# Where the wide tiles of a two-layer decoder trunk stand in SBUF: multiples of 512 bytes, with the small tiles together in front

## The chip, the cores and the metric

The kernel runs on one core of a Trainium2 chip. The metric is the device time of one launch in microseconds (us). The three runs of the kernel before took 2445.65, 2446.26 and 2448.31 us; their median is 2446.26 us.

## What is computed

Two decoder layers on 1,024 tokens of width 1,024, all in float32. Cut to what matters:

```python
proj = x @ w_in                                   # 1024 x 3592 columns
fq, fk, fv, f_logit, rq, rk, rv, rg = split(proj) # f_logit has 8 columns
fox = attention(fq, fk, fv, bias=cumsum(log_sigmoid(f_logit + b)))   # 8 heads of 64, causal
ret = silu(rg) * groupnorm(retention(rotary(rq), rotary(rk), rv))    # 4 heads of 128, chunks of 128
x = layernorm(ALPHA * x + concat(fox, ret) @ w_out)
x = layernorm(ALPHA * x + square(relu(x @ w_ff1)) @ w_ff2)           # hidden width 4096
```

## The kernel before

**Products of float32 in three passes.** Each operand of a large matmul is split into a high part (`hi`, an ACT cast at line 152) and a remainder (`lo`, a DVE subtraction at line 153). `mm3` (line 211) and the two `product` functions (`triple` at line 1053 belongs to the second) then issue three matmuls for every 128 rows of contraction: lo·hi, hi·lo and hi·hi. Each matmul has a stationary operand of 128 x 128, which a weight load brings in before it, and a moving operand of 256, 264 or 512 columns.

**The stages of a layer, with their pools.**

- `p1`: value projection (`project_values`: 256 columns with weights `va`, then 264 columns with weights `vb`, that is 256 values and the 8 forget logits), `forget_sums`, then `retention` for two pairs of heads, each with four projections of 256 columns. In these the weights move and the tokens are stationary. Last comes the first of four pairs of `project_qk`, where the weights are stationary and 512 tokens move.
- `p2`: attention, with the other three pairs of `project_qk` woven between its steps.
- `p3`: the output projection with `w_out` (512 columns, `mm3`) and the first layer norm.
- `p3` and `p4`: `feed_forward_in`, 16 blocks of seven half-size products of 12 matmuls each (a Strassen-like scheme), 512 columns, line 843: 16 x 7 x 12 = 1,344 matmuls a layer, 2,688 in all. The stationary operand is a weight in `whi` or `wlo`, the moving one is `xop`.
- `p5`: `feed_forward_out`, the same count of matmuls at line 1053, both operands from the pair `ehi`, `elo`.

`mm3` issues 1,536 matmuls of 512 columns: 2 layers x 4 pairs x 2 names x 2 halves x 24 = 768 in `project_qk`, and 2 layers x 2 halves x 8 token tiles x 24 = 768 for `w_out`. Of the 768 in `project_qk`, 2 x 96 are in `p1` and 2 x 288 in `p2`.

**The weights' ring.** `load_next` fetches one block of weights into a staging tile `wst` (two buffers) and splits it into `whi` and `wlo` (four buffers each). All blocks share these tiles, so that each buffer has the size of the largest one: `vb` with 4 x 264 columns, 4,224 bytes in each partition; every other block has 4,096 bytes or less. `weight` asks for a block and emits the next two (`AHEAD`).

**Order.** The order of the instructions on each engine is set by a planner that simulates the program; a buffer's next user waits until the last one is done with it. Pools `p1` to `p5` use the same room one after the other (`reuse_waits="tile"`: a tile waits only for the tiles that stood where it stands). All DMA issues but one kind go through SP's queue, in order.

**Addresses.** Tiles stand one behind the other in the order of the pools and of their first use, each size rounded up to 32 bytes. In the built program of the kernel before these are the bytes in a partition at which they start:

| tile | starts at | remainder by 256 |
|---|---|---|
| `cst`, `half` (8 bytes) | 1152, 3968 | 128, 128 |
| `act`, 11 buffers of 8,192 (tokens, `mix`, most of `xop`) | 4000 + 8192 n | 160 |
| `wst`, 2 buffers of 4,224 | 94112, 98336 | 160, 32 |
| `whi`, 4 buffers of 4,224 | 102560, 106784, 111008, 115232 | 160, 32, 160, 32 |
| `wlo`, 4 buffers of 4,224 | 119456, 123680, 127904, 132128 | 160, 32, 160, 32 |
| `p1` to `p5`; in `p3` the other `xop` | from 140448 | 160 |
| `ehi` and `elo` of `p5`, 6 buffers of 4,096 each | 157216 + 4096 n | 32, 32 |

Matmuls run on TensorE in the order of the program, so that each one of the trace can be given its addresses. Three products of 12 matmuls at line 843 in layer 1, by the time at which their first one starts in the trace:

| first matmul | moving `xop` | stationary `whi`, `wlo` | remainders by 256 |
|---|---|---|---|
| 2004.57 us | 61344, 44960 | 111008, 127904 | 160 and 160 |
| 2007.30 us | 4000, 36768 | 108832, 125728 | 160 and 32 |
| 2010.09 us | 69536, 12192 | 115232, 132128 | 160 and 32 |

(The product at 2007.30 uses the second half of its weights' tiles. Each of the three stretches has 12 matmuls, up to the next line or up to 2012.88 us. In a tile of weights each further 128 columns start 512 bytes later, in `xop` each further 512 columns 2,048 bytes later, which leaves the remainders as they are.)

In the 256-column projections of layer 0 the same can be done: of the matmuls of 256 columns, those from 98.21 us to 99.64 us move `whi` and `wlo` with remainder 32 past stationary tokens with 160, those from 99.64 us to 101.06 us with remainder 160 past 160, and then again 32 past 160.

Of the kernel before, what the change touches and what calls it, by code (L numbers as in the profile page):

```python
# [9 lines left out]
F32 = mybir.dt.float32  # L10
# [7 lines left out]
P = 128  # L18
# [21 lines left out]
LEAD_ORDER = (0, None, 1, None, 2, None, 3, None, 0, 1, 2, 3, 4, 5, 4, 5)  # L40
SPAN = 3.0
ACT_SLOTS = 11
RING = 4
# [31 lines left out]
def hybrid_trunk(ctx: ExitStack, tc, x, w_in, w_out, w_ff1, w_ff2, ln1_g, ln1_b, ln2_g, ln2_b,  # L75
# [3 lines left out]

    cp = ctx.enter_context(tc.tile_pool(name="cp", bufs=1))  # L80
    act = ctx.enter_context(tc.tile_pool(name="act", bufs=ACT_SLOTS))
    wp = ctx.enter_context(tc.tile_pool(name="wp", bufs=RING))
# [15 lines left out]
    V.tensor_copy(mbf, cst[:, 384:512])  # L98
    half = cp.tile([P, 2], F32, tag="half", name="half")
    V.memset(half, -0.5)  # L100

    q_d = dp.tile([FH, 2, FD, S], F32R, tag="q_d", name="q_d")
# [82 lines left out]
    place = {k: n for n, k in enumerate(order)}  # L185
    loaded, emitted = {}, [0]

    def load_next(after=None):
        key = order[emitted[0]]
        emitted[0] += 1  # L190
        src = specs[key]
        _, kk, cc = src.shape
        st = wp.tile([P, kk, cc], F32, tag="wst", name=nm("wst"), bufs=2)
        if after is not None:
            V.tensor_copy(st[0:1, 0, 0:1], after)
        SP.dma_start(st, src)
        hi = wp.tile([P, kk, cc], F32R, tag="whi", name=nm("whi"))
        lo = wp.tile([P, kk, cc], F32R, tag="wlo", name=nm("wlo"))
        split(hi, lo, st)
        loaded[key] = (hi, lo)  # L200
# [48 lines left out]

    def rstd_of(pool, mv, n):  # L250
        sd = pool.tile([P, n], F32, tag="sd", name=nm("sd"), bufs=2)
        G.tensor_scalar(sd, mv[:, :, 1], EPS, 1.0, op0=ALU.add, op1=ALU.mult)
        rs = pool.tile([P, n], F32, tag="rs", name=nm("rs"), bufs=2)
        G.tensor_tensor(rs, sd, half[:, 0:n], op=ALU.pow)
        nb = pool.tile([P, n], F32, tag="nb", name=nm("nb"), bufs=2)
        V.scalar_tensor_tensor(nb, mv[:, :, 0], -1.0, rs, op0=ALU.mult, op1=ALU.mult)
        return rs, nb

    def layernorm(pool, z, st, g, b):
        mv = pool.tile([P, 1, 2], F32, tag="mv", name=nm("mv"), bufs=2)  # L260
        V.bn_aggr(mv[:, 0, :], st)  # L261
        V.scalar_tensor_tensor(z, z, mv[:, 0, 0:1], g, op0=ALU.subtract, op1=ALU.mult)
        sd = pool.tile([P, 1], F32, tag="sd", name=nm("sd"), bufs=2)
        G.tensor_scalar(sd, mv[:, :, 1], EPS, 1.0, op0=ALU.add, op1=ALU.mult)  # L264
        rs = pool.tile([P, 1], F32, tag="rs", name=nm("rs"), bufs=2)
        G.tensor_tensor(rs, sd, half[:, 0:1], op=ALU.pow)
        V.scalar_tensor_tensor(z, z, rs, b, op0=ALU.mult, op1=ALU.add)

    def layernorm_halves(pool, z, st, g, b, dst):
        mv = pool.tile([P, 1, 2], F32, tag="mv", name=nm("mv"), bufs=2)  # L270
        V.bn_aggr(mv[:, 0, :], st)
        rs, nb = rstd_of(pool, mv, 1)
# [13 lines left out]

    def project_values(l, xT, pool, prepare):
        wv = [weight(l, "va", g) for g in range(2)]
# [18 lines left out]
        wv = [weight(l, "vb", g) for g in range(2)]  # L307
        bf = pool.tile([P, FH], F32, tag="bf", name=nm("bf"), bufs=1)
        SP.dma_start(bf, rows(b_forget[l], P))
        z = pool.tile([P, NT, FH], F32, tag="z", name=nm("z"), bufs=1)  # L310
        for tt in range(NT):
# [3 lines left out]
            V.tensor_tensor(z[:, tt, :], ps[:, 256:264], bf, op=ALU.add)  # L315
        return z

# [33 lines left out]
    def retention(l, r, xT, pool, cos, sin, gn, steps):  # L351
# [77 lines left out]
        def outputs(tp, j, vt, inner):  # L429
            tt = 2 * tp + j  # L430
            po = ps_pv.tile([P, 512], F32, tag="pv", name=nm("pv"))
            for h in range(2):
                hs = slice(h * P, h * P + P)
                PE.matmul(po[:, hs], inner[:, hs], vt[:, j, h, :], start=True, stop=tt == 0)
                if tt > 0:
                    PE.matmul(po[:, hs], qT[tp][:, h, j, :], states[tt][:, hs], start=False, stop=True)
            st = pool.tile([P, 2, 6], F32, tag="rst", name=nm("rst"), bufs=2)
            mv = pool.tile([P, 2, 2], F32, tag="rmv", name=nm("rmv"), bufs=2)
            for h in range(2):
                V.bn_stats(st[:, h, :], po[:, h * P : h * P + P])  # L440
                V.bn_aggr(mv[:, h, :], st[:, h, :])
            rs, nb = rstd_of(pool, mv, 2)
# [42 lines left out]
    def attention(pool, mixes, fill, need, take):  # L485
# [15 lines left out]
        def load_bias(h):  # L501
            ncb = pool.tile([P, S], F32, tag="ncb", name=nm("ncb"), bufs=1)
            SP.dma_start(ncb, rows(c_d[h], P))
            ref = pool.tile([P, 4], F32, tag="ref", name=nm("ref"), bufs=2)
            G.tensor_scalar(ref, ncb.rearrange("p (a b) -> p a b", b=256)[:, :, 0], -1.0, 1.0, op0=ALU.mult, op1=ALU.mult)
            sums[h] = (ncb, ref)
# [8 lines left out]
        def front(h, qq, probs):  # L515
# [3 lines left out]
            for rb in (2 * qq, 2 * qq + 1):  # L519
# [5 lines left out]
                for c0 in range(0, nw, cw):  # L525
# [10 lines left out]
                    m2 = pool.tile([P, 1], F32, tag="mx", name=nm("mx"), bufs=6)  # L536
# [5 lines left out]
                sm = pool.tile([P, 1], F32, tag="sm", name=nm("sm"), bufs=4)  # L542
                A.activation(sc[:, 0:ne], sc[:, 0:ne], AF.Exp, bias=mx, scale=-1.0, accum_out=sm)
                ri = pool.tile([P, 1], F32, tag="ri", name=nm("ri"), bufs=4)
                V.reciprocal(ri, sm)
# [95 lines left out]
    def layer(l, xT, nxt):  # L641
        src = x if l == 0 else x_d
        with tc.tile_pool(name=f"p1_{l}", bufs=1, reuse_waits="tile") as pool:
# [26 lines left out]
            SP.dma_start(gn, rows(ret_gn_g[l].rearrange("h d -> (h d)"), P))  # L670
            z = project_values(l, xT, pool, prepare)
            forget_sums(z, pool)
            steps = [0]
            for r in range(2):
                retention(l, r, xT, pool, cos, sin, gn, steps)
            for _ in project_qk(l, 0, xT):
                pass
            settle()
        mix = {}
# [40 lines left out]
        with tc.tile_pool(name=f"p3_{l}", bufs=1, reuse_waits="tile") as outer:  # L720
# [3 lines left out]
            with tc.tile_pool(name=f"p3a_{l}", bufs=1, reuse_waits="tile") as pool:  # L724
                acc = []
                for tt in range(NT):
# [7 lines left out]
                    acc.append(a)  # L734
                gT = pool.tile([P, 8], F32, tag="gT", name=nm("gT"))
                bT = pool.tile([P, 8], F32, tag="bT", name=nm("bT"))
                SP.dma_start(gT, ln1_g[l].rearrange("(k p) -> p k", p=P))
                SP.dma_start(bT, ln1_b[l].rearrange("(k p) -> p k", p=P))
                stats = pool.tile([P, NT, 2, 6], F32, tag="stats", name=nm("stats"))

# [17 lines left out]
                def norm(tt):  # L758
                    mv = pool.tile([P, 1, 2], F32, tag="mv", name=nm("mv"), bufs=2)
                    V.bn_aggr(mv[:, 0, :], stats[:, tt])  # L760
                    rs, nb = rstd_of(pool, mv, 1)
                    A.activation(acc[tt], acc[tt], AF.Identity, bias=nb, scale=rs)
# [250 lines left out]
    def feed_forward_out(l, operands, nxt):  # L1013
# [10 lines left out]

        stats = keep.tile([P, NT, 2, 6], F32, tag="stats2", name=nm("stats2"))
        acc = {}
# [54 lines left out]
        def finish(tt):  # L1081
# [4 lines left out]
            if nxt is None and tt == NT - 1:  # L1086
                layernorm_halves(keep, zt, stats[:, tt], g, b, out[tt * P : tt * P + P, :])
                return
            layernorm(keep, zt, stats[:, tt], g, b)
            if nxt is None:  # L1090
# [71 lines left out]
```

## Time and profile before

| | |
|---|---|
| median of 3 runs | 2446.26 us |
| the profiled execution's own time | 2446.42 us |
| span of its instructions | 2444.6 us |
| PE (matmuls) busy | 2395.4 us, 98% |
| DVE, ACT, POOL busy | 62%, 42%, 15% |
| DMA | 442.68 MB, mean 181 GB/s |

The span runs from the first to the last instruction; 1.8 us of the profiled time lie around it. A matmul counts as busy from its start to its modelled end, and a matmul starts before the one ahead of it has ended: at 512 columns the mean of one is some 390 ns, while starts follow each other at some 230 ns. What a matmul costs is therefore read from the distance of the starts, or from a stretch in which PE has no gap, divided by the number of matmuls in it.

### The profile page before, as it was taken

Reading aid. Unit: us, or ns where it says so; the run is one execution under the profiler, and the core shown is the slowest. Engines: PE = TensorE matmul, PEld = TensorE weight load, DVE = VectorE, ACT = ScalarE, POOL = GpSimd, SP = SyncE. Lnnn points to the kernel's source line nnn. Section 1 sums busy time; section 2 is a strip of 40 time slices with the busy share of each in tenths; the row PEclk is TensorE's granted clock in tenths of the full one; section 3 lists DMA queues with packets and bytes.
Section 4 is the critical chain, followed back from the end, with each engine's and each line's share of the span. In section 5 each row is a group of like instructions: output and inputs, shape, how many; then the busy total and the mean of one; then the engine's idle time right before and its main releaser. Section 6 shows DMA issues by size and latency. Waiting matters only on the chain. (4 is left out here: it accounts for less than half of the span.)

```text
span 2444.6 us, 35615 instructions
## 1 busy us (share of the span) xinstructions
PE 2395.4 (98%) x13424; PEld 2063.4 (84%) x13424; DVE 1521.2 (62%) x2720; ACT 1019.7 (42%) x1540; POOL 376.2 (15%) x661
## 2 busy tenths in 40 slices
PE   8999999999999999999999999999999999999997
PEld 8999977787788888888899998877877888888886
DVE  4655447854876667665755554577557766576557
ACT  3212246734544454334321222477264444443331
POOL 0324224600000000000203332245000000000003
PEclk9999999999999999999999999999999999999998
DMA  6555675433364458667545567664334544586664
GB/s 212 174 211 199 211 225 167 136 108 121 100 213 156 142 185 306 207 211 222 171 151 190 190 225 234 177 172 112 117 104 146 182 159 162 193 303 215 198 191 146
DMA packets 243309, 442.68 MB, mean 181 GB/s; under 512 B 25520, under 2 KB 127920, under 8 KB 234944
## 3 DMA queue, kind: packets, MB, share of 16 engines
q1 hardware_dynamic: 240832, 432.01, 54.0%
q10 hardware_dynamic: 2304, 8.39, 0.9%
q8 instruction: 106, 1.74, 0.3%
q14 instruction: 67, 0.55, 0.1%
HBM read 301.85 MB, written 138.48 MB: 180 GB/s over the span
## 5 line engine op out<-in xcount | busy, mean ns | idle before, releaser
L153 DVE TENSOR_TENSOR elo<-est,ehi 128x1024 fp32r<-128x1024 f32 x216 | 261.2, 1222 | 183.0 <-ACT ehi L152 182.2
L152 ACT CAST ehi<-est 128x1024 fp32r<-128x1024 f32 x216 | 226.6, 1054 | 343.8 <-PE pv L1053 120.8
L211 PE MATMUL mm<-whi,act 128*128 128x256 f32 (+2 forms) x1376 | 274.4, 293 | 1.0 <-DVE act L153 0.5
L211 PE MATMUL qk<-whi,act 128*128 128x256 f32 (+2 forms) x1376 | 273.1, 292 | 0.8 <-DVE act L153 0.8
L211 PEld LDWEIGHTS mm<-whi,act 128*128 128x128 f32 x1376 | 220.5, 191 | 5.5 <-ACT whi L152 0.8
L211 PEld LDWEIGHTS qk<-whi,act 128*128 128x128 f32 x1376 | 218.3, 189 | 4.6 <-DVE act L153 1.0
L152 ACT CAST whi<-wst 128x1024 fp32r<-128x1024 f32 (+2 forms) x156 | 132.4, 852 | 170.2 <-PE qk L211 55.6
L211 PE MATMUL mm<-wlo,act 128*128 128x256 f32 (+2 forms) x688 | 200.9, 292 | 0.7 <-DVE wlo L153 0.7
L264 POOL TENSOR_SCALAR sd<-mv 128x1 f32<-128x1 f32 x15 | 13.6, 908 | 1221.4 <-DVE mv L261 1221.1
L211 PE MATMUL qk<-wlo,act 128*128 128x256 f32 (+2 forms) x688 | 199.3, 290 | 0.0
L843 PE MATMUL qk<-xop,whi 128*128 128x512 f32 x608 | 189.8, 393 | 0.0
L153 DVE TENSOR_TENSOR wlo<-wst,whi 128x1024 fp32r<-128x1024 f32 (+2 forms) x156 | 153.0, 984 | 46.3 <-ACT whi L152 43.9
L211 PE MATMUL mm<-act,whi 128*128 128x512 f32 x512 | 166.4, 398 | 0.0
L843 PE MATMUL pv<-xop,whi 128*128 128x512 f32 x512 | 159.5, 393 | 0.0
L582 PE MATMUL pv<-pt,vp 128*128 128x256 f32 x640 | 130.9, 307 | 8.2 <-POOL pt L564 5.8
L843 PEld LDWEIGHTS qk<-xop,whi 128*128 128x128 f32 x608 | 114.5, 188 | 26.0
L211 PEld LDWEIGHTS mm<-wlo,act 128*128 128x128 f32 x688 | 131.2, 191 | 2.8 <-DVE wlo L153 1.0
L211 PEld LDWEIGHTS qk<-wlo,act 128*128 128x128 f32 x688 | 130.0, 189 | 1.6
L843 PE MATMUL mm<-xop,whi 128*128 128x512 f32 x384 | 119.5, 392 | 1.5 <-DVE xop L153 1.5
L152 ACT CAST pt<-tr 128x512 fp32r<-128x512 f32 (+1 forms) x160 | 85.7, 538 | 84.5 <-PE tr L559 79.6
L153 DVE TENSOR_TENSOR pt<-tr,pt 128x512 fp32r<-128x512 f32 (+1 forms) x160 | 99.8, 631 | 32.8 <-ACT pt L152 31.9
L843 PE MATMUL qk<-xop,wlo 128*128 128x512 f32 x304 | 120.1, 395 | 0.0
(260 smaller groups left out, 5628.8 us busy)
## 6 DMA issues: line engine op xcount, KB each, us to landing
est<-h_d SPq DMA_DIRECT2D x224, 256.0 KB, 3.7
wst<-in_w_ff_dram SPq DMA_DIRECT2D x76, 512.0 KB, 4.2
wr<-in_w_ff_dram SPq DMA_DIRECT2D x32, 1024.0 KB, 5.9
t_d<-ts SPq DMA_DIRECT2D x32, 1024.0 KB, 4.1
h_d<-hs SPq DMA_DIRECT2D x32, 1024.0 KB, 5.1
est<-t_d SPq DMA_DIRECT2D x128, 256.0 KB, 3.7
wst<-in_w_in_dram SPq DMA_DIRECT2D x52, 512.0 KB, 5.1
h_d<-rest SPq DMA_DIRECT2D x32, 768.0 KB, 5.6
```

The lines of the kernel that those rows point to most:

```text
L152: A.copy(hi, src)
L153: V.tensor_tensor(lo, src, hi.bitcast(F32), op=ALU.subtract)
L211: PE.matmul(ps, lhs(a, k), rhs(b, k), start=first and i == 0 and j == 0, stop=last and i == n - 1 and j == 2)
L264: G.tensor_scalar(sd, mv[:, :, 1], EPS, 1.0, op0=ALU.add, op1=ALU.mult)
L582: PE.matmul(ob[:, (qq % 2) * 256 : (qq % 2) * 256 + 256], vp[:, j, :], pt[b][:, 2 * i : 2 * i + 2, :], start=qq % 2 == 0 and jp == 0 and i ...
L843: PE.matmul(ps, ops[p][a][:, k, :], right[p][b][:, k, :], start=first and k == 0 and n == 0, stop=last and k == 3 and n == 2, skip_group_c ...
```

## The change

- The small tiles, those of 8 to 384 bytes (`sd`, `rs`, `nb`, `mv`, `rst`, `rmv`, `ref`, `mx`, `sm`, `ri`, `bf`, `gT`, `bT`, `stats`), leave the pools of the stages for a pool `sp` of their own, which stands ahead of `act` and lives as long as the kernel. The two `stats` become one.
- `half` gets 224 bytes in place of 8. With the sizes above, the tiles in front of `act` then end at byte 5,632 = 11 x 512 (1152 + 2304 + 256 + 256 + 224 for the constants, 1,440 for `sp`).
- The blocks `vb` no longer go through the ring: they get a staging tile `vst` of one buffer and tiles `vhi0`, `vlo0`, `vhi1`, `vlo1`, in a pool `p1v` that lives during `project_values` only. The ring's buffers shrink to 4,096 bytes. So `act`, `wst`, `whi`, `wlo`, `ev` and the pools `p1` to `p5` all start at multiples of 512.
- `p1` keeps `cos`, `sin`, `gn`, `z` (256 bytes) and `vt`; what `forget_sums` and `retention` use goes into a pool `p1r`, in the room of `p1v`. Both start 256 bytes past a multiple of 512. In `p1r` seven tiles of 256 bytes come first, so that its wide tiles stand at multiples of 512; those of `p1v` do not.

No instruction of any engine is added or taken away by the text of the program, and none changes its size.

```diff
+HALF_ROOM = 56
...
+    sp = ctx.enter_context(tc.tile_pool(name="sp", bufs=1))
     act = ctx.enter_context(tc.tile_pool(name="act", bufs=ACT_SLOTS))
     wp = ctx.enter_context(tc.tile_pool(name="wp", bufs=RING))
...
-    half = cp.tile([P, 2], F32, tag="half", name="half")
+    half = cp.tile([P, HALF_ROOM], F32, tag="half", name="half")[:, 0:2]
     V.memset(half, -0.5)
+
+    def small(shape, tag, bufs=2):
+        return sp.tile(shape, F32, tag=tag, name=nm(tag), bufs=bufs)
...
-        st = wp.tile([P, kk, cc], F32, tag="wst", name=nm("wst"), bufs=2)
+        odd = key[1] == "vb"
+        home, two = (odd_home[0], 1) if odd else (wp, 2)
+        tags = ("vst", f"vhi{key[2]}", f"vlo{key[2]}") if odd else ("wst", "whi", "wlo")
+        st = home.tile([P, kk, cc], F32, tag=tags[0], name=nm(tags[0]), bufs=two)
         if after is not None:
             V.tensor_copy(st[0:1, 0, 0:1], after)
         SP.dma_start(st, src)
-        hi = wp.tile([P, kk, cc], F32R, tag="whi", name=nm("whi"))
-        lo = wp.tile([P, kk, cc], F32R, tag="wlo", name=nm("wlo"))
+        hi = home.tile([P, kk, cc], F32R, tag=tags[1], name=nm(tags[1]))
+        lo = home.tile([P, kk, cc], F32R, tag=tags[2], name=nm(tags[2]))
         split(hi, lo, st)
...
-            st = pool.tile([P, 2, 6], F32, tag="rst", name=nm("rst"), bufs=2)
-            mv = pool.tile([P, 2, 2], F32, tag="rmv", name=nm("rmv"), bufs=2)
+            st = small([P, 2, 6], "rst")
+            mv = small([P, 2, 2], "rmv")
...
-            z = project_values(l, xT, pool, prepare)
-            forget_sums(z, pool)
-            steps = [0]
-            for r in range(2):
-                retention(l, r, xT, pool, cos, sin, gn, steps)
-            for _ in project_qk(l, 0, xT):
-                pass
-            settle()
+            z = pool.tile([P, NT, FH], F32, tag="z", name=nm("z"), bufs=1)
+            with tc.tile_pool(name=f"p1v_{l}", bufs=1, reuse_waits="tile") as odd_home[0]:
+                project_values(l, xT, pool, prepare, z)
+            with tc.tile_pool(name=f"p1r_{l}", bufs=1, reuse_waits="tile") as part:
+                forget_sums(z, part)
+                steps = [0]
+                for r in range(2):
+                    retention(l, r, xT, part, cos, sin, gn, steps)
+                for _ in project_qk(l, 0, xT):
+                    pass
+                settle()
...
-        stats = keep.tile([P, NT, 2, 6], F32, tag="stats2", name=nm("stats2"))
+        stats = small([P, NT, 2, 6], "stats", 1)
```

The remaining lines of the diff are of these kinds: a small tile is taken from `small`, and functions lose the argument `pool` for it.

## Rows read from the trace of the kernel before

**Rows 1.** The page: the span, and busy time of each engine.

```profile
span 2444.6 us, 35615 instructions
PE 2395.4 (98%) x13424; PEld 2063.4 (84%) x13424; DVE 1521.2 (62%) x2720; ACT 1019.7 (42%) x1540; POOL 376.2 (15%) x661
```

**Rows 2.** Waits of PE: in all, times, longest, in us.

```profile
PE tr L236 <- DMA xs<-in_x_dram: 6.1, 2, 5.0
PE pv L582 <- POOL pt L564: 5.8, 10, 1.2
PE mm L211 <- DVE ev L156: 3.5, 2, 1.9
```

**Rows 3.** Windows: length, busy us and instructions of each engine, granted clock, DMA.

```profile
740.00:880.00 140.00, 140.00 (x609) 114.18 (x607) 90.69 (x131) 68.69 (x104) 0.00 (x0) 1.00 0.41 145
1000.00:1140.00 140.00, 140.00 (x620) 115.91 (x619) 84.06 (x91) 55.45 (x53) 0.00 (x0) 1.00 0.66 200
1940.00:2080.00 140.00, 140.00 (x608) 114.17 (x607) 91.57 (x133) 67.23 (x101) 0.00 (x0) 1.00 0.45 162
2220.00:2360.00 140.00, 140.00 (x619) 115.96 (x618) 78.13 (x79) 53.96 (x52) 0.00 (x0) 1.00 0.68 206
```

**Rows 4.** Timeline of PE at line 843: start, length, engine, line, tiles.

```profile
2004.57 0.39 PE L843 MATMUL qk<-xop,wlo 128*128 128x512 f32 x1
...
2007.30 0.40 PE L843 MATMUL qk<-xop,wlo 128*128 128x512 f32 x1
...
2010.09 0.39 PE L843 MATMUL tr<-xop,wlo 128*128 128x512 f32 x1
...
2012.88 0.39 PE L843 MATMUL tr<-xop,wlo 128*128 128x512 f32 x1
```

**Rows 5.** Timeline of PE in the projections of 256 columns.

```profile
98.33 0.28 PE L211 MATMUL qk<-wlo,act 128*128 128x256 f32 x1
...
99.76 0.28 PE L211 MATMUL qk<-wlo,act 128*128 128x256 f32 x1
...
101.18 0.28 PE L211 MATMUL qk<-wlo,act 128*128 128x256 f32 x1
```

**Rows 6.** Windows, line 211 on PE alone, in the output projection.

```profile
535.00:575.00 40.00, 40.00 (x175) 1.00 0.42 144
```

**Rows 7.** Windows, PE alone, in the attention of either layer.

```profile
330.00:530.00 200.00, 192.14 (x1195) 1.00 0.48 135
1530.00:1740.00 210.00, 201.96 (x1236) 1.00 0.50 141
```

**Rows 8.** Timeline of SP and ACT: the first weights of layer 1.

```profile
1154.50 1.55 SPq L196 DMA_DIRECT2D wst<-in_w_in_dram  x2
1160.86 0.38 SPq L196 DMA_DIRECT2D wst<-in_w_in_dram  x1
1158.46 1.08 ACT L152 CAST whi<-wst 128x1056 fp32r<-128x1056 f32 x1 [2.38 <-DMA wst<-in_w_in_dram]
```

**Rows 9.** Timeline of PE: last matmul of layer 0, first with `vb`.

```profile
1221.25 0.40 PE L1053 MATMUL pv<-ehi 128*128 128x512 f32 x1
...
1249.98 0.28 PE L211 MATMUL mm<-whi,act 128*128 128x264 f32 x1
```

**Rows 10.** The page's DMA issues (us to landing), and a split of `vb`.

```profile
wst<-in_w_in_dram SPq DMA_DIRECT2D x52, 512.0 KB, 5.1
1159.57 1.26 DVE L153 TENSOR_TENSOR wlo<-wst,whi 128x1056 fp32r<-128x1056 f32 x1 [1.66 <-ACT whi L152]
```

**Rows 11.** Windows at the seam of the layers, all engines.

```profile
1217.00:1239.00 22.00, 20.58 (x153) 19.09 (x152) 20.79 (x31) 5.28 (x10) 5.49 (x8) 1.00 0.37 118
1239.00:1250.00 11.00, 11.00 (x95) 11.00 (x94) 1.46 (x4) 1.64 (x2) 0.00 (x0) 1.00 0.50 172
```

More of the change, by code (lines that the diff above doesn't have):

```diff
@@ L185, in hybrid_trunk @@
     place = {k: n for n, k in enumerate(order)}
-    loaded, emitted = {}, [0]
+    loaded, emitted, odd_home = {}, [0], [None]
     def load_next(after=None):
@@ L248, in transpose_half, with rstd_of, layernorm, layernorm_halves @@
             yield kk
-    def rstd_of(pool, mv, n):
-        sd = pool.tile([P, n], F32, tag="sd", name=nm("sd"), bufs=2)
+    def rstd_of(mv, n):
+        sd = small([P, 2], "sd")[:, 0:n]
         G.tensor_scalar(sd, mv[:, :, 1], EPS, 1.0, op0=ALU.add, op1=ALU.mult)
-        rs = pool.tile([P, n], F32, tag="rs", name=nm("rs"), bufs=2)
+        rs = small([P, 2], "rs")[:, 0:n]
         G.tensor_tensor(rs, sd, half[:, 0:n], op=ALU.pow)
-        nb = pool.tile([P, n], F32, tag="nb", name=nm("nb"), bufs=2)
+        nb = small([P, 2], "nb")[:, 0:n]
         V.scalar_tensor_tensor(nb, mv[:, :, 0], -1.0, rs, op0=ALU.mult, op1=ALU.mult)
         return rs, nb
-    def layernorm(pool, z, st, g, b):
-        mv = pool.tile([P, 1, 2], F32, tag="mv", name=nm("mv"), bufs=2)
+    def layernorm(z, st, g, b):
+        mv = small([P, 1, 2], "mv")
         V.bn_aggr(mv[:, 0, :], st)
         V.scalar_tensor_tensor(z, z, mv[:, 0, 0:1], g, op0=ALU.subtract, op1=ALU.mult)
-        sd = pool.tile([P, 1], F32, tag="sd", name=nm("sd"), bufs=2)
+        sd = small([P, 2], "sd")[:, 0:1]
         G.tensor_scalar(sd, mv[:, :, 1], EPS, 1.0, op0=ALU.add, op1=ALU.mult)
-        rs = pool.tile([P, 1], F32, tag="rs", name=nm("rs"), bufs=2)
+        rs = small([P, 2], "rs")[:, 0:1]
         G.tensor_tensor(rs, sd, half[:, 0:1], op=ALU.pow)
         V.scalar_tensor_tensor(z, z, rs, b, op0=ALU.mult, op1=ALU.add)
-    def layernorm_halves(pool, z, st, g, b, dst):
-        mv = pool.tile([P, 1, 2], F32, tag="mv", name=nm("mv"), bufs=2)
+    def layernorm_halves(z, st, g, b, dst):
+        mv = small([P, 1, 2], "mv")
         V.bn_aggr(mv[:, 0, :], st)
-        rs, nb = rstd_of(pool, mv, 1)
+        rs, nb = rstd_of(mv, 1)
         h0, h1 = slice(0, D // 2), slice(D // 2, D)
@@ L284, in rows, with project_values @@
         return ap.partition_broadcast(n)
-    def project_values(l, xT, pool, prepare):
+    def project_values(l, xT, pool, prepare, z):
         wv = [weight(l, "va", g) for g in range(2)]
@@ L307, in project_values @@
         wv = [weight(l, "vb", g) for g in range(2)]
-        bf = pool.tile([P, FH], F32, tag="bf", name=nm("bf"), bufs=1)
+        bf = small([P, FH], "bf", 1)
         SP.dma_start(bf, rows(b_forget[l], P))
-        z = pool.tile([P, NT, FH], F32, tag="z", name=nm("z"), bufs=1)
         for tt in range(NT):
@@ L441, in outputs @@
                 V.bn_aggr(mv[:, h, :], st[:, h, :])
-            rs, nb = rstd_of(pool, mv, 2)
+            rs, nb = rstd_of(mv, 2)
             on = pool.tile([P, 256], F32, tag="on", name=nm("on"), bufs=2)
@@ L503, in load_bias @@
             SP.dma_start(ncb, rows(c_d[h], P))
-            ref = pool.tile([P, 4], F32, tag="ref", name=nm("ref"), bufs=2)
+            ref = small([P, 4], "ref")
             G.tensor_scalar(ref, ncb.rearrange("p (a b) -> p a b", b=256)[:, :, 0], -1.0, 1.0, op0=ALU.mult, op1=ALU.mult)
@@ L535, in front @@
                         PE.matmul(ps[:, o : o + P], ibf, mbf, start=False, stop=True)
-                    m2 = pool.tile([P, 1], F32, tag="mx", name=nm("mx"), bufs=6)
+                    m2 = small([P, 1], "mx", 6)
                     V.tensor_tensor_reduce(out=sc[:, c0 : c0 + we], in0=ps[:, 0:we], in1=rel[:, c0 : c0 + we], scale=-1.0,
@@ L541, in front @@
                         yield
-                sm = pool.tile([P, 1], F32, tag="sm", name=nm("sm"), bufs=4)
+                sm = small([P, 1], "sm", 4)
                 A.activation(sc[:, 0:ne], sc[:, 0:ne], AF.Exp, bias=mx, scale=-1.0, accum_out=sm)
-                ri = pool.tile([P, 1], F32, tag="ri", name=nm("ri"), bufs=4)
+                ri = small([P, 1], "ri", 4)
                 V.reciprocal(ri, sm)
@@ L734, in layer @@
                     acc.append(a)
-                gT = pool.tile([P, 8], F32, tag="gT", name=nm("gT"))
-                bT = pool.tile([P, 8], F32, tag="bT", name=nm("bT"))
+                gT = small([P, 8], "gT", 1)
+                bT = small([P, 8], "bT", 1)
                 SP.dma_start(gT, ln1_g[l].rearrange("(k p) -> p k", p=P))
                 SP.dma_start(bT, ln1_b[l].rearrange("(k p) -> p k", p=P))
-                stats = pool.tile([P, NT, 2, 6], F32, tag="stats", name=nm("stats"))
+                stats = small([P, NT, 2, 6], "stats", 1)
                 def turn(hf):
@@ L758, in norm @@
                 def norm(tt):
-                    mv = pool.tile([P, 1, 2], F32, tag="mv", name=nm("mv"), bufs=2)
+                    mv = small([P, 1, 2], "mv")
                     V.bn_aggr(mv[:, 0, :], stats[:, tt])
-                    rs, nb = rstd_of(pool, mv, 1)
+                    rs, nb = rstd_of(mv, 1)
                     A.activation(acc[tt], acc[tt], AF.Identity, bias=nb, scale=rs)
@@ L1023, in affine @@
             return g, b
-        stats = keep.tile([P, NT, 2, 6], F32, tag="stats2", name=nm("stats2"))
+        stats = small([P, NT, 2, 6], "stats", 1)
         acc = {}
@@ L1086, in finish @@
             if nxt is None and tt == NT - 1:
-                layernorm_halves(keep, zt, stats[:, tt], g, b, out[tt * P : tt * P + P, :])
+                layernorm_halves(zt, stats[:, tt], g, b, out[tt * P : tt * P + P, :])
                 return
-            layernorm(keep, zt, stats[:, tt], g, b)
+            layernorm(zt, stats[:, tt], g, b)
             if nxt is None:
```

1 line of the change is left out of this document (removed).

## Prediction

> **What bounds the kernel now.** I read the page first: PE has matmuls in flight for 98% of the span, and no other engine is above 62% [rows 1]. The waits of PE come next: the longest kind sums to 6.1 us, at the very start, and the largest others are of 5.8 and 3.5 us [rows 2]. So the time is PE's own rate, and a change of where tiles stand can gain only if it changes that rate, and lose only if it makes PE wait.
>
> So the third view is windows, 140 us long, in the two feed-forward stages, where PE has no gap [rows 3]. Both stages issue the same matmul, 128 x 128 by 512 columns. In `feed_forward_in` a window holds 609 and 608 of them, in `feed_forward_out` 620 and 619. A matmul that reaches over the edge is counted in both windows, so I divide 140.39 us by the count: 230.5 and 230.9 ns against 226.4 and 226.8 ns. On average that is 230.7 against 226.6, or 4.1 ns each. The granted clock is 1.00 in all four. The faster stage moves more over DMA (share 0.66 and 0.68 against 0.41 and 0.45), so traffic does not explain the difference.
>
> The timeline inside `feed_forward_in` shows what does [rows 4]. Three stretches of 12 matmuls of the same line, engines and shapes take 2.73, 2.79 and 2.79 us: 227.5 ns each in the first, 232.5 in the other two. By the table of addresses, the first reads moving and stationary operand from starts with the same remainder by 256 (160 and 160), the others from different ones (160 and 32). In `feed_forward_out` both stand at 32, and it runs at the fast rate throughout. So neither remainder is slow by itself; equal is fast, unequal slow. The mean of 230.7 is a mixture, because the buffers of the ring are 4,224 bytes = 16.5 x 256 apart and alternate between the two remainders.
>
> **The change, part by part.**
>
> *Equal remainders at line 843.* Every wide tile but `vb` then starts at a multiple of 512, so all pairs are equal, as in `feed_forward_out`. I take its rate: 2,688 x 4.1 ns = **11.0 us** less [rows 3]. The bounds: 0 if the remainder is not the cause, and 11.6 at the fastest window's 226.4 ns, below which no row goes.
>
> *Equal remainders at 512 columns of `mm3`.* Half the ring's buffers again stand against tokens at 160. In the output projection 175 matmuls take 40.39 us, 230.8 ns, so 4.2 ns above the fast rate [rows 3, 6]. For the 768 of `w_out` and the 192 of `project_qk` in `p1`, where PE is dense, that is 960 x 4.2 = **4.0 us**. The other 576 lie in attention, where PE is busy 96% [rows 7] and some of what they save is waited away at the next step of the softmax. At 4.2 ns they are worth 2.4 us; I take half, **1.2 us**, with 0 and 2.4 as bounds.
>
> *256 and 264 columns.* In the projections 12 matmuls with unequal remainders take 1.43 us and 12 with equal ones 1.42 us: 119 ns either way [rows 5]. I cost this at **0**. The weights `vb` keep odd starts, and their 264 columns are in the same regime: 0. The transposes against `cst` (which stays at 1152) and the retention's matmuls are 128 columns, nearer to rows 5 than to rows 4: 0, with 1 us either way.
>
> *A pool for small tiles.* It removes some reuse waits on DVE and POOL, which have spare time [rows 1]: 0.
>
> *`vb` in tiles of its own.* In layer 0 `vst` waits for nothing. In layer 1 the cover shrinks. Before, the ring was free, and the last block of `vb` was cast at 1158.46 us [rows 8], 91 us ahead of its first use at 1249.98 us [rows 9]. Now `vst` and `vhi0` stand on the room of `est` and the first buffers of `ehi` in `p5`. By the order in which the ring is filled, one of these is read by the last group of four blocks, hence until the last matmul of layer 0 at 1221.25 us [rows 9]. From there one block takes 5.1 us to land, 1.08 for the cast and 1.26 for the subtraction [rows 8, 10], 7.4 us; the second waits for the single `vst`, so both are there after 14.9 us, at 1236.4 us, 13.6 us before their use. What is queued behind them: on SP the stores of layer 0's last rows and the tables for rotary, which are needed later; on ACT and DVE the evictions of transposed tokens, which PE needs at once. DVE is busy 20.79 of 22 us there [rows 11], so its two subtractions (2.5 us) may push an eviction back. PE already loses 22.0 - 20.58 = 1.4 us at that place. I take **+1.0 us**, with 0 and 4.7 (both casts and subtractions, 2 x 2.34, all in front of PE's evictions) as bounds.
>
> *The planner's order.* Freed ring buffers let `rq` be fetched earlier, and the planner may arrange other steps anew. The trace cannot show it. All of PE's idle time is 2444.6 - 2395.4 = 49 us [rows 1], so I allow a tenth of it, 5 us, either way, and take 0.
>
> Sum: -11.0 - 4.0 - 1.2 + 1.0 = -15.2 us on the profiled execution's own 2446.42 us (span 2444.6 and 1.8 around it), that is 2431.2. The median of the runs is 2446.26, 0.16 us lower; I say **2431 us**, 0.6% less.
>
> A rule of the Trainium skill speaks against this. The page "SBUF — State Buffer", section "Who interferes with whom", gives PE two independent read ports, one for the moving operand and one for the weight load, and says "PE and ACT never wait on anyone". By that rule the place of one operand against the other could not matter, and the sum would be 0: 2446 us. Rows 4 disagree with it, 227.5 against 232.5 ns in one stage, and the measurement decides; no run here yet changes the address alone.
>
> **The rivals.**
>
> *No change of rate: 2446 us (2443 to 2449).* The fast and slow stretches would differ by something that goes with the tile and not with its start, for example how lately DVE wrote it. For it: `feed_forward_in` has more DVE and ACT work than `feed_forward_out` (90.69 and 68.69 against 84.06 and 55.45 us in 140) [rows 3]. Against it: rows 4 switch rate exactly where the remainder switches, within 10 us of the same mixture of work.
>
> *The gain is given back in part: 2434 to 2441 us.* PE gets ahead of the splits and of attention's chain, or the seam costs its 4.7 us and the new order 5 more. For it: DVE at the seam [rows 11]. Against it: DVE and ACT have a third and half of `feed_forward_in` free [rows 3], and PE's gain is under 2%.
>
> *Slower: remainder 0 is the slow case.* Every fast stretch has both starts 32 bytes past a multiple of 128; nothing shows two starts at 0. If the reads then met at each step, all 512-column matmuls would run at 232.5 ns: 2 x 2,688 x 232.5 against 2,688 x (230.7 + 226.6) is +20.7 us, and 1,536 x 1.7 makes +2.6: 2470 us. It decides once the new rate is above 229.1 ns, the mean over all 6,912 of these matmuls now (2,688 at 230.7, 2,688 at 226.6, 1,536 at 230.8). Against it: equal remainders of 160 and of 32 are both fast.
>
> *Better still: under 2424 us.* The whole 2.4 us in attention, no loss at the seam and 5 us by a better order give 2424; a rate below 226.4 ns is on no row.
>
> **How the numbers follow.** Chances: forecast as summed (2425 to 2434) 0.68; given back in part 0.14; no change of rate 0.08; slower, by remainder 0 or by a seam and an order far worse than bounded, 0.07; better than 2425, 0.03. The first two make 0.82; their bounds are 2424 (the sum with every gain) and 2441, and that is the range. A measurement of this kernel can tell about 0.2%, or 4.9 us, from no change. The first two and the last fall under 2441.4, and a little of the "no change" case does too: faster 0.86; same 0.07; slower 0.07.
>
> **What would show it.** In the profile after: windows of 140 us in `feed_forward_in` should hold 619 or 620 matmuls, as `feed_forward_out` does, which itself stays as it is; products of 12 should all take 2.72 to 2.73 us; 256 columns stay at 119 ns. At the seam the load of `vb` should be issued after the last matmul of layer 0 and PE's idle time between the layers should grow by no more than some us. I am wrong if windows in `feed_forward_in` still hold 609, if `feed_forward_out` slows down, or if PE's waits grow by 10 us or more while its rate improves.

## The result, and the profile after

The changed kernel takes **2431.8 us** (median of 6 runs, 2428.72 to 2434.84), the kernel before 2446.5 in the same comparison (6 runs, 2445.09 to 2448.57). The ratio is 0.9938 with a 95% interval of 0.9925 to 0.9951: faster by 0.6%, where 2431 (2424 to 2441) was forecast. The profiled execution took 2434.84 us, 11.6 less than the profiled one before (2446.42). In the code after, line 843 is 853, 1053 is 1063, 211 is 220, 152 and 153 are 158 and 159, and 582 is 589.

The page of the changed kernel, span and busy time [rows 1]:

```profile
span 2433.1 us, 35602 instructions
PE 2383.8 (98%) x13424; PEld 2065.2 (85%) x13424; DVE 1520.0 (62%) x2720; ACT 1019.9 (42%) x1540; POOL 376.1 (15%) x661
```

PE (TensorE, which runs the matmuls; DVE, ACT and POOL are VectorE, ScalarE and GpSimd) is still the bound at 98%, with the same 13,424 matmuls; it is busy for 11.6 us less, and the span is 11.5 us shorter. So the matmuls themselves became faster, as the windows show. Windows of the changed kernel, in the columns of [rows 3], two in each feed-forward stage:

```profile
740.00:880.00 140.00, 140.00 (x620) 115.95 (x619) 91.87 (x136) 68.95 (x105) 0.00 (x0) 1.00 0.43 155
1000.00:1140.00 140.00, 140.00 (x620) 115.95 (x619) 80.97 (x85) 55.71 (x53) 0.00 (x0) 1.00 0.68 206
1930.00:2070.00 140.00, 140.00 (x619) 115.93 (x618) 92.89 (x135) 69.26 (x104) 0.00 (x0) 1.00 0.46 165
2210.00:2350.00 140.00, 140.00 (x620) 115.95 (x619) 76.73 (x78) 54.77 (x52) 0.00 (x0) 1.00 0.68 206
```

`feed_forward_in` (first and third row) now holds 620 and 619 matmuls where it held 609 and 608; `feed_forward_out` is as it was. The granted clock is 1.00 in all, before and after. The timeline of PE in the changed kernel, with the first matmuls of two products and of the one behind them [rows 4]:

```profile
2000.28 0.39 PE L853 MATMUL tr<-xop,wlo 128*128 128x512 f32 x1
...
2003.00 0.39 PE L853 MATMUL tr<-xop,wlo 128*128 128x512 f32 x1
...
2005.72 0.39 PE L853 MATMUL pv<-xop,wlo 128*128 128x512 f32 x1
```

Twelve matmuls take 2.72 us each time; the stretches of 2.79 us are gone. The output projection, line 220 on PE alone, in the columns of [rows 6]:

```profile
535.00:575.00 40.00, 40.00 (x179) 1.00 0.40 149
```

Here 179 matmuls start where 175 did. Not everything gained. The stretch from 232 to 252 us holds only matmuls of 256 columns in either kernel; first the kernel before, then the changed one:

```profile
232.00:252.00 20.00, 20.00 (x171) 1.00 0.58 205
```

```profile
232.00:252.00 20.00, 20.00 (x169) 1.00 0.58 198
```

With the 0.28 us of the one at the edge that is 20.28/171 = 118.6 ns before and 20.28/169 = 120.0 ns after: these became slower.

For the whole run I add up, in each trace, the distances from the start of a matmul to the start of the next, by line and width. Waits are in these sums.

| matmuls | before, us | after, us | difference | forecast |
|---|---|---|---|---|
| `feed_forward_in`, 2,688 | 627.3 | 616.7 | -10.6 | -11.0 |
| `mm3`, 512 columns, 1,536 | 364.6 | 361.0 | -3.6 | -5.2 |
| `mm3`, 256 columns, 3,456 | 421.1 | 424.0 | +2.9 | 0 |
| `feed_forward_out`, 2,687 | 609.4 | 609.7 | +0.2 | 0 |
| all others | | | -0.4 | +1.0 |
| all | | | -11.5 | -15.2 |

The seam of the layers, SP's queue in the changed kernel [rows 8 to 10]:

```profile
1220.03 9.02 SPq L1103 DMA_DIRECT2D x_d<-acc  x4
1229.14 0.39 SPq L675 DMA_DIRECT2D cos<-rope_dram  x1
...
1231.95 0.43 SPq L205 DMA_DIRECT2D vst<-in_w_in_dram  x1
...
1240.30 0.37 SPq L205 DMA_DIRECT2D vst<-in_w_in_dram  x1
```

DVE's subtractions for the two blocks, and PE's last matmul of layer 0 and first with `vhi`:

```profile
1239.02 1.26 DVE L159 TENSOR_TENSOR vlo<-vst,vhi 128x1056 fp32r<-128x1056 f32 x1 [5.05 <-ACT vhi L158]
...
1245.70 1.26 DVE L159 TENSOR_TENSOR vlo<-vst,vhi 128x1056 fp32r<-128x1056 f32 x1 [4.83 <-ACT vhi L158]
```

```profile
1215.59 0.39 PE L1063 MATMUL pv<-ehi 128*128 128x512 f32 x1
...
1244.44 0.28 PE L220 MATMUL mm<-vhi,act 128*128 128x264 f32 x1
```

The load of the first block left 16.4 us after the last matmul of layer 0, behind the stores of layer 0's last rows and the rotary tables, and the blocks were split by 1240.28 and 1246.96 us, the first 4.2 us ahead of the first matmul that needs it. PE paid nothing: the windows of 50 us around the seam, before and after, at the same place of the work, are

```profile
1215.00:1265.00 50.00, 48.58 (x379) 46.74 (x378) 27.12 (x43) 10.25 (x19) 5.49 (x8) 1.00 0.43 143
```

```profile
1210.00:1260.00 50.00, 48.62 (x380) 46.90 (x379) 28.98 (x45) 12.27 (x21) 5.49 (x8) 1.00 0.49 159
```

and PE's only waits in either are one of 0.8 and one of 0.5 us for DVE's tokens `act`.

### The profile page after: what moved, and what is told of

It is laid out like the page before. It is cut to its first block, busy times and chain, and to the rows that moved or that the text cites. A ratio compares the mean times of both kernels' runs of the same rounds, so it can differ in the third digit from the quotient of the medians.

```text
span 2433.1 us, 35602 instructions
## 1 busy us (share of the span) xinstructions
PE 2383.8 (98%) x13424; PEld 2065.2 (85%) x13424; DVE 1520.0 (62%) x2720; ACT 1019.9 (42%) x1540; POOL 376.1 (15%) x661
## 3 DMA queue, kind: packets, MB, share of 16 engines
q10 hardware_dynamic: 2304, 8.39, 0.8%
## 5 line engine op out<-in xcount | busy, mean ns | idle before, releaser
L220 PE MATMUL mm<-whi,act 128*128 128x256 f32 (+1 forms) x1248 | 251.0, 295 | 0.8 <-DVE act L159 0.5
L220 PE MATMUL qk<-whi,act 128*128 128x256 f32 (+1 forms) x1248 | 249.8, 294 | 0.8 <-DVE act L159 0.8
L220 PEld LDWEIGHTS mm<-whi,act 128*128 128x128 f32 x1248 | 202.1, 193 | 5.1 <-DVE act L159 0.8
L220 PEld LDWEIGHTS qk<-whi,act 128*128 128x128 f32 x1248 | 200.2, 191 | 4.4 <-DVE act L159 1.0
L158 ACT CAST whi<-wst 128x1024 fp32r<-128x1024 f32 (+1 forms) x152 | 128.3, 847 | 161.5 <-PE qk L220 46.7
L220 PE MATMUL mm<-wlo,act 128*128 128x256 f32 (+1 forms) x624 | 183.5, 294 | 0.7 <-DVE wlo L159 0.7
L220 PE MATMUL qk<-wlo,act 128*128 128x256 f32 (+1 forms) x624 | 181.9, 292 | 0.0
L159 DVE TENSOR_TENSOR wlo<-wst,whi 128x1024 fp32r<-128x1024 f32 (+1 forms) x152 | 148.2, 978 | 38.8 <-ACT whi L158 36.4
L220 PEld LDWEIGHTS mm<-wlo,act 128*128 128x128 f32 x624 | 120.6, 193 | 2.7 <-DVE wlo L159 1.0
L220 PEld LDWEIGHTS qk<-wlo,act 128*128 128x128 f32 x624 | 119.5, 191 | 1.5
L853 PE MATMUL qk<-xop,wlo 128*128 128x512 f32 x304 | 118.6, 390 | 0.0
```

Source lines behind the costliest of these rows:

```text
L158: A.copy(hi, src)
L159: V.tensor_tensor(lo, src, hi.bitcast(F32), op=ALU.subtract)
L220: PE.matmul(ps, lhs(a, k), rhs(b, k), start=first and i == 0 and j == 0, stop=last and i == n - 1 and j == 2)
L853: PE.matmul(ps, ops[p][a][:, k, :], right[p][b][:, k, :], start=first and k == 0 and n == 0, stop=last and k == 3 and n == 2, skip_group_c ...
```

## The experiments

**The theory:** a matmul of 512 columns runs at some 227 ns when the byte addresses of its moving and its stationary operand are equal by 256, and slower when they are not; nothing else of the change matters. **The rivals:** it is the multiple of 512 itself that helps; it is the pool for small tiles, or the new order of the work. Later a second question came up, what the places do at 256 columns. Times stand beside runs of the kernel before on the same chip: 2445.37 us (median of 20) for the first four kernels, 2446.53 (15) for the next four, 2445.6 (11) for the last three. Windows are of PE alone, 740 to 880 us (`feed_forward_in`) unless another stretch is named; columns are length, busy us and matmuls, granted clock, DMA share, GB/s. Where bytes are named, they come from the addresses in the built program.

**Everything 32 bytes past a multiple of 512.**

```diff
-HALF_ROOM = 56
+HALF_ROOM = 64
```

> The changed kernel with 32 bytes more in front of act: every wide tile starts 32 bytes past a multiple of 512, and the order of all instructions stays. Theory A (the remainders by 256 of the moving and the stationary operand must be equal): 140 us of feed_forward_in hold 619 or 620 matmuls as now, 2432 us (2429 to 2435). Theory B (the tiles must stand at multiples of 512): the rate falls back to that of the kernel before, 609 in 140 us, 2446 us. Open beside it: the 256-column matmuls take about 1 ns more in the changed kernel than before (3,456 of them, some 3 us); if that comes from starts at remainder 0, it goes away here and the time is 2429 us.

Measured: 2436.2 us (9 runs, 2434.73 to 2440.68), ratio 0.9963 (0.9951 to 0.9975).

```profile
740.00:880.00 140.00, 140.00 (x619) 1.00 0.40 145
```

The rate is that of the changed kernel: `feed_forward_in` sums to 617.0 us against 616.7. No wide tile stands at a multiple of 512, so that rival falls. The 4 us between this median and the changed kernel's may be noise: in the repeat on this chip, further down, the changed kernel took 2433.73 us, with an interval that overlaps this one. In the two profiles the difference is not in the rate; it lies in `mm3` at 512 columns in and around attention (176.6 us for `w_out` against 176.4, 188.5 for `project_qk` against 184.5), where waits are included. PE's wait for `ev` at the hand-over from `p1` to `p2` (in all, times, longest) and the window from 319 to 325 us behind it, here and then in the changed kernel:

```profile
PE mm L220 <- DVE ev L162: 4.8, 2, 2.6
319.00:325.00 6.00, 6.00 (x14) 0.50 1.02 246
```

```profile
PE mm L220 <- DVE ev L162: 3.6, 2, 2.0
319.00:325.00 6.00, 6.00 (x28) 1.00 1.02 245
```

So here PE waited 1.2 us longer, and behind the wait, at a granted clock of 0.50, 14 matmuls started where 28 did. The missing 14 are worth 14 x 0.229 = 3.2 us, an estimate from these rows and the 229 ns of dense starts in `project_qk`. The two together come to about the 4 us; why the wait was longer, these runs do not show.

**`vb` in tiles of its own, and nothing else.** The kernel before, with these lines of the change; the small tiles stay in their stages' pools, and tokens, ring and pools start 416 bytes past a multiple of 512, remainder 160.

```diff
+        odd = key[1] == "vb"
+        home, two = (odd_home[0], 1) if odd else (wp, 2)
+        tags = ("vst", f"vhi{key[2]}", f"vlo{key[2]}") if odd else ("wst", "whi", "wlo")
...
+            with tc.tile_pool(name=f"p1v_{l}", bufs=1, reuse_waits="tile") as odd_home[0]:
+                project_values(l, xT, pool, prepare, z)
```

> The kernel before with one part of the change alone: vb in tiles of its own, so that the ring's buffers are 4,096 bytes; the small tiles stay where they were. act, the ring and the pools then start at 416 past a multiple of 512 (remainder 160 by 256), nothing wide stands at a multiple of 512. Theory A: all pairs equal, 619 or 620 matmuls in 140 us, the whole gain, 2431 us (2428 to 2435). Theory B: 609 in 140 us, 2446 us. Theory C (the gain comes from the pool of small tiles, by fewer waits): 2446 us.

Measured: 2436.37 us (6 runs, 2431.91 to 2438.33), ratio 0.9958 (0.9941 to 0.9974), an interval that overlaps the changed kernel's.

```profile
740.00:880.00 140.00, 140.00 (x619) 1.00 0.43 155
```

Sums: 616.9 us for `feed_forward_in`, 361.7 for `mm3` at 512 columns, 423.0 at 256. This part alone, which makes the ring's buffers 16 x 256 bytes in place of 16.5, gives the whole change of rate. What the small tiles' pool adds to it is not told from nothing.

**The weights moved against the rest.** The changed kernel, with a tile of `SHIFT` bytes between `wst` and `whi` and one of `256 - SHIFT` behind `wlo`, so that only the weights move. Four sizes, 128, 64, 32 and 96:

```diff
+        if not odd and not padded:
+            padded.append(pad("pad1", SHIFT))
         hi = home.tile([P, kk, cc], F32R, tag=tags[1], name=nm(tags[1]))
         lo = home.tile([P, kk, cc], F32R, tag=tags[2], name=nm(tags[2]))
+        if not odd and len(padded) == 1:
+            padded.append(pad("pad2", 256 - SHIFT))
```

> The changed kernel with 128 bytes of padding between the staging tiles and whi, and 128 behind wlo: the weights' ring stands at remainder 128 by 256, everything else at 0. Theory A: every matmul of feed_forward_in and of mm3 is unequal; 2,688 x 5.9 ns = 15.9 us and 1,536 x 5.9 ns less what attention hides, 6 to 9 us, on 2432: 2455 us, slower than the kernel before (2446), with 603 to 605 matmuls in 140 us of feed_forward_in and still 620 in feed_forward_out. Theory B: half the operands stand at multiples of 512, so between 2432 and 2446. If the address does not matter: 2432.

> The same with 64 and 192 bytes of padding: the ring at remainder 64, the rest at 0. If any unequal pair is slow: as with 128, 603 to 605 matmuls in 140 us. If only the distance of 128 is slow: 619 or 620.

> The weights' ring at remainder 32, everything else at 0. Theory A (only equal is fast at 512 columns): 601 to 605 matmuls of feed_forward_in in 140 us. If reads are told apart by lines of 64 bytes, 32 counts as equal and it holds 619 or 620. The 256-column matmuls, which went from 424.0 us in all (remainder equal) to 419.6 (128 apart) and 415.3 (64 apart): between 415 and 424.

> The weights' ring at remainder 96, everything else at 0. Theory A: 601 to 605 matmuls of feed_forward_in in 140 us; if 32 and 96 differ from 64 and 128, the rule is one of steps of 64. The 256-column matmuls: between 415 and 424 us.

At 128 it took 2449.86 us (10 runs), ratio 1.002 (1.0008 to 1.0031): a little slower than before the change. The other three ran once: 2447.14 (64), 2448.51 (32) and 2461.19 us (96). `feed_forward_in` and `feed_forward_out` at 128:

```profile
740.00:880.00 140.00, 140.00 (x601) 1.00 0.40 145
1000.00:1140.00 140.00, 140.00 (x619) 1.00 0.65 200
```

The stage whose operands were moved apart falls to 601 matmuls, (140 + 0.39)/601 = 233.6 ns; the one whose operands both stay where they were keeps 619. At 64, 32 and 96 the first row holds 602, 601 and 600. So any of the four distances costs, and in this stage about the same. Mean distances of starts over the whole run, gaps beyond 260 ns (145 ns at 256 columns) left out:

| weights past tokens by | `feed_forward_in`, ns | `w_out`, ns | `mm3` 256 columns, ns | its sum, us |
|---|---|---|---|---|
| 0 (changed kernel) | 226.8 | 227.6 | 119.9 | 424.0 |
| 32 | 233.3 | 233.2 | 116.9 | 414.0 |
| 64 | 233.3 | 230.7 | 117.6 | 415.3 |
| 96 | 234.3 | 233.4 | 119.9 | 424.1 |
| 128 | 233.2 | 232.4 | 118.8 | 419.6 |

The last columns were the surprise: at 256 columns equal places are not the fast case. 32 bytes apart saves 10 us there. This is also why three of the four did not come out as slow as their matmuls of 512 columns would make them: at 128, +16.9 us in `feed_forward_in` and +3.0 in `mm3` at 512 columns (against the changed kernel) stand against -4.4 at 256. At 96 nothing is given back, +19.7 and +7.0 against +0.1, and it is the slowest.

**Only the 256-column weights apart.** If 512 columns want equality and 256 want distance, blocks of 256 columns can start some bytes into their buffer. Buffers of 4,352 bytes (17 x 256), with `APART` = 16 floats (64 bytes), and as a control the same program with `APART` = 0. To make room, attention's tile `rl` shares the buffer of `ev2`.

```diff
+            o = APART if cc == 256 else 0
+            hi, lo = (home.tile([P, 1088], F32R, tag=g, name=nm(g))[:, o : o + 1024].rearrange("p (k c) -> p k c", c=cc)
+                      for g in tags[1:])
...
-            t = pool.tile([P, RH * RD], F32, tag="rl", name=nm("rl"), bufs=1)
+            t = pool.tile([P, RH * RD], F32, tag="ev2", name=nm("rl"), bufs=1)
```

> A version meant to beat both kernels: in the changed kernel the ring's buffers for whi and wlo get 4,352 bytes (17 x 256); blocks of 256 columns stand 64 bytes into their buffer, all others at its start. The room comes from rl, which shares a tile with ev2. Theory: 512 columns keep equal remainders (619 or 620 in 140 us), 256 columns get the 415.3 us of the ring at 64 in place of 424.0: 8.7 us less, 2424 us on the chip where the changed kernel takes 2432, that is 0.9910 of the kernel before. If the 256-column matmuls were faster there for another reason (the order of the pools, the padding): 0.994 to 0.996.

> The same with all blocks at the start of their buffers; instructions and their order are the same. Theory: as the changed kernel, 0.994 to 0.996 of the kernel before, 256 columns 423 to 424 us in all, 8.7 us or 0.35% above the one with 64 bytes. If the two agree within 0.1%, the 64 bytes do nothing.

Measured: 2437.99 us apart (5 runs, 2435.97 to 2441.47), ratio 0.9965 (0.9953 to 0.9978), and 2443.7 without (11 runs, 2439.11 to 2447.06), ratio 0.9986 (0.9977 to 0.9995). The stretch from 232 to 252 us, 64 bytes apart and then equal:

```profile
232.00:252.00 20.00, 20.00 (x173) 1.00 0.64 230
```

```profile
232.00:252.00 20.00, 20.00 (x169) 1.00 0.56 201
```

In both, the ring's buffers, 17 x 256 bytes each, stand by turns 0 and 256 bytes past a multiple of 512, the tokens at 0. `feed_forward_in` sums to 617.1 and 616.9 us, the rate of the changed kernel, so a distance of 256 bytes counts as equal: it is the remainder by 256 that matters, and not that by 512. The sums at 256 columns are 417.1 and 424.4 us; the 7.3 between them is the distance's own worth, in the same instruction order, and the medians stand 5.7 apart. Both lost more than that to what they have in common: the matmuls of probabilities and values (line 589 of the changed kernel) sum to 115.0 and 114.8 us in place of 106.0. PE's waits 64 bytes apart:

```profile
PE pv L595 <- POOL pt L577: 11.2, 13, 1.7
```

In the control this kind sums to 11.2 too, in the changed kernel to 5.9. So both came out slower than was expected of them. Whether the shared buffer or the larger ones make POOL late was not separated.

**A version with all at its better place.** High and low part of a block in one tile of 8,448 bytes (33 x 256), 256-column blocks 32 bytes into it, so that no tile of attention need be shared. Room comes from `cst`, whose mask goes through `ev` at the start. Beside it, on the same chip, the changed kernel again.

```diff
+    def pair(n, apart=0):
+        t = wp.tile([P, 2112], F32R, tag="whl", name=nm("whl"))
+        return t[:, apart : apart + n], t[:, apart + n : apart + 2 * n]
...
+            hi, lo = (t.rearrange("p (k c) -> p k c", c=cc) for t in pair(kk * cc, APART if cc == 256 else 0))
```

> Another version meant to beat both, without touching attention: hi and lo of a block share one tile of 8,448 bytes (33 x 256), in which blocks of 256 columns stand 32 bytes further on and all others at the start; the room comes from the 512 bytes of the causal mask in cst, which is read into ev once, and all wide tiles stand at remainder 224. Theory: 512 columns equal, 619 or 620 in 140 us; 256 columns at 32 apart, 414 us in all as measured with the ring at 32, 10 us less than the changed kernel: 0.990 of the kernel before. If the shared tile makes the lo and hi parts wait for each other: 0.994 or above.

> The changed kernel itself, beside the last one on the same chip. All theories: 0.9938 of the kernel before, within its interval of 0.9925 to 0.9951.

Measured: 2430.63 us (6 runs, 2427.26 to 2437.56), ratio 0.9943 (0.993 to 0.9956), against 2433.73 (5 runs, 2431.49 to 2435.52), ratio 0.9952 (0.9941 to 0.9964). The intervals overlap: not told apart. The 256 columns gave what the distance promises, 413.4 against 424.3 us (the changed kernel's figures here are those of this second profile of it). But `mm3` at 512 columns took 366.2 against 358.7. Its waits at the hand-over from `p1` to `p2` grew, and the clock fell behind them; PE's wait for `ev` (in all, times, longest), in this version and in the changed kernel:

```profile
PE mm L228 <- DVE ev L163: 6.4, 2, 3.7
```

```profile
PE mm L220 <- DVE ev L162: 2.9, 2, 1.6
```

One such wait in the timeline of this version, and then the window from 314 to 321 us in it and in the changed kernel:

```profile
315.79 6.40 PE L228 MATMUL mm<-act,whl 128*128 128x512 f32 x16 [3.69 <-DVE ev L163]
```

```profile
314.00:321.00 7.00, 5.21 (x12) 0.52 1.05 251
```

```profile
314.00:321.00 7.00, 5.73 (x26) 1.00 0.94 326
```

After PE had stood still for 3.69 us, its matmuls were granted 0.52 of full speed, about the lower of its two levels (1.2 of 2.4 GHz); in the changed kernel's second profile, where this wait was 1.27 us, the clock stayed at 1.00. The DMA engines are as good as full in this place in both (shares of 1.05 and 0.94). That PE came there earlier because of its faster projections is not reason enough: with the weights moved by 32 bytes PE came there at 313.2 us, in this version at 312.1 and in the changed kernel at 317.5, and it waited 1.48 us:

```profile
314.69 0.50 PE L231 MATMUL mm<-act,wlo 128*128 128x512 f32 x1 [1.48 <-DVE ev L163]
```

Why the wait is longer in this version stays open. Nor does the length of the wait settle by itself whether the clock falls. At the same hand-over in layer 1 PE waited 1.99 us in the first profile of the changed kernel and 2.15 us in the kernel of the next experiment. The 5 us behind these waits, in this order:

```profile
1521.00:1526.00 5.00, 4.61 (x13) 0.66 1.00 268
```

```profile
1524.00:1529.00 5.00, 4.84 (x21) 1.00 1.03 257
```

**Only the low parts moved.** The changed kernel with the tile of 128 bytes between `whi` and `wlo`.

> The changed kernel with wlo alone at remainder 128, whi and everything else at 0: of three matmuls at line 843 the first is stationary in wlo, the other two in whi. If a matmul is slowed by its own stationary operand's place, or by that of the next one, whose load runs beside it, one of three starts is late: 140 us hold about 613 (a third of the way from 620 to 601). Which matmul is followed by a longer distance tells the two apart: the first of three (own), or the third (next).

Measured: 2444.0 us (one run).

```profile
740.00:880.00 140.00, 140.00 (x607) 1.00 0.40 145
```

Not the 613 that one slow matmul in three would make, but 607: two in three are slow. The timeline of PE and of its weight loads (PEld) in this kernel, over twelve matmuls:

```profile
799.82 0.40 PE L864 MATMUL tr<-xop,wlo 128*128 128x512 f32 x1
800.05 0.62 PE L864 MATMUL tr<-xop,whi 128*128 128x512 f32 x2
800.28 0.19 PEld L864 LDWEIGHTS tr<-xop,wlo 128*128 128x128 f32 x1
...
802.59 0.40 PE L864 MATMUL tr<-xop,wlo 128*128 128x512 f32 x1
```

Twelve take 2.77 us, between 2.72 and 2.79. By the distances of the starts over the whole run, a matmul with `wlo` (its own operands apart) takes 234.1 ns. One with `whi` that is followed by `wlo` (its own equal, the next one's weights apart) takes 232.5, and one with `whi` followed by `whi` 227.0. In the changed kernel the same three are 227.0, 226.7 and 226.6 ns, so it is not the order of the three that does it. A matmul is slowed by its own weights' place and by the next one's. The next ones are loaded while it runs: above, `wlo` from 800.28 us on, when the second matmul with `whi` starts. Its own were loaded before it, so why their place counts these rows do not show. That only its own or only the next one's place matters fell here. At 256 columns, where the weights move, this kernel's mean is 117.5 ns: less than with all weights equal (119.9) and with all 128 apart (118.8).

## Why the prediction was right, point by point

*PE's own rate is the bound, and the places set it: shown.* The part of the change that alters the ring's buffer size, and it alone, gives the fast windows; moving the weights takes them away without touching `feed_forward_out`; moving everything by 32 bytes leaves them. The reading of [rows 4], equal fast and unequal slow, held for each distance tried.

*Line 843, -11.0 us: measured -10.6.* Windows of 619 and 620, products of 2.72 us, as named beforehand.

*512 columns of `mm3`, -5.2: measured -3.6.* `w_out` gave 178.9 - 176.4 = 2.5 us where 768 x 4.2 = 3.2 were counted, since the equal rate there is 227.6 ns and not 226.6. The rest, about 1.2 of 2.0, lies in `project_qk`. There the rate itself moved less than the 4.2 ns that were counted: from 230.4 to 227.7 ns in `p1` and from 230.9 to 229.5 in attention (gaps beyond 260 ns left out). That some of the gain in attention was waited away, as assumed, is not shown. Two profiles of the same changed kernel differ by 2.3 us in this sum (361.0 and 358.7, that is 3.6 and 5.9 us less than before), so the miss is hardly larger than that.

*256 columns, 0: measured +2.9, the term that was mis-sized.* [Rows 5] compared one equal stretch of 12 with its unequal neighbours, 1.42 against 1.43 us. In a mixture both come out near 118.9 ns over the whole run; all equal, it is 119.9 (changed kernel), all 128 apart 118.8. An equal stretch between unequal ones does not show the rate of an equal one that goes on. Why the equal ones of the mixture run at 118.9 stays open; that a mixture can be faster than either kind alone, the last experiment shows too. The rule that unequal is slow was right to be left out here, but the opposite sign was not considered.

*`vb` at the seam, +1.0: measured 0.* The direction was right and its size harmless: the cover was thinner than I said, because the loads wait in SP's queue for the stores of layer 0's last rows, which I had put behind them. The load left 16.4 us after the last matmul of layer 0, more than the whole slack of 13.6 that I counted. The second block was ready 2.5 us after the first use of the first one (1246.96 against 1244.44); PE did not wait, so the two are not needed at once.

*Small tiles and order, 0 with 5 either way:* nothing of 5 us is seen; the intervals of the kernel with `vb` alone and of the changed kernel overlap.

*The sum.* By the sums of the traces -11.5 us was measured and -15.2 forecast. The miss of 3.7 is 1.6 for `mm3` at 512 columns, 2.9 for 256 columns, 0.4 for line 843 and 0.2 for `feed_forward_out`, less 1.4 for the remaining matmuls with the seam. The median of the runs (2431.8) is 3.0 below the profiled one, so that it came within 1 us of 2431. Of that agreement some is luck: in the repeat the same kernel took 2433.73 us, 11.9 less than before on that chip and not the 15.2 of the sum. The mechanism was right; the sum was too large.

*The rivals.* "No change of rate" fell: moving the weights alone by 32 to 128 bytes took `feed_forward_in` from 226.8 to 233 or 234 ns. With it fell what the prediction drew from the Trainium skill (the page "SBUF — State Buffer", section "Who interferes with whom"), that two independent read ports would leave the places no part in the time. "Remainder 0 is the slow case" fell for 512 columns. For 256 columns it has its grain of truth, since equal is slower than 32 or 64 apart, yet equal at 32 (the first experiment, 119.9 ns) is as slow as equal at 0. "Given back in part" holds to the extent of the 2.9 us.

## What to carry to other kernels

Where PE is the bound at a granted clock of 1.00, look at the distance of matmul starts by the byte addresses of both operands before looking for waits: one tile larger than the rest in a ring of buffers can put every second buffer at another remainder. Compare long stretches in which all pairs are alike, and try each width by itself, because what is fast at 512 columns was not fast at 256. Count a gain of rate where PE stays dense: one version here gained 10.9 us in its projections and took 7.5 us more in `mm3` at 512 columns, beside longer waits at a hand-over where the DMA engines are full and a lower clock behind them.

## What was not expected of the hardware

- At 512 columns in this three-pass float32, any distance tried (32, 64, 96, 128 bytes by 256) between moving and stationary starts costs 3 to 8 ns over 226.8 to 227.6. At 256 columns the best of those tried is 32 bytes apart, 116.9 against 119.9 ns, over 3,456 matmuls 10 us. A distance of 256 bytes costs nothing at 512 columns (616.9 us for the stage, against 616.7).
- The slow-down follows the place of the next stationary operand as well as of the matmul's own (232.5 and 234.1 against 227.0 ns).
- After a wait of 3.69 us at one place the granted clock was 0.52 over 7 us, the end of the wait among them, and 12 matmuls started where 26 did; after one of 1.27 us there it stayed at 1.00. The length of the wait does not settle it alone: at the same hand-over in layer 1 the clock fell behind a wait of 1.99 us and stayed at 1.00 behind one of 2.15 us, in two kernels.
